# One decoder layer on one core: x handed in by features, without transposes on TensorE

## The chip, the cores and the metric

The kernel runs on one core of a Trainium2 chip. The metric is the device time of one execution in microseconds (us), as the median of several runs. Beside it there is one execution taken by the hardware profiler, with every instruction of every engine: TensorE (PE, with its weight loads as PEld), VectorE (DVE), ScalarE (ACT), GpSimd (POOL) and SyncE (SP). SP, ACT and POOL also issue the transfers between the chip's memory (HBM) and the on-chip memory (SBUF). TensorE writes its products to PSUM.

## What is computed

One layer of a decoder on 512 tokens of width 2048, in float32:

```
h = rmsnorm(x, ln_mix)
proj = h @ w_in                       # 2048 -> 4608: sb_q sb_k sb_v sw_q sw_k sw_v
sb_o = stick_breaking_attention(sb_q, sb_k, sb_v)        # 16 heads, causal
sw_o = sliding_window_sink_attention(sw_q, sw_k, sw_v, sinks, slopes)
x = x + concat(rmsnorm(sb_o, sb_out_norm), rmsnorm(sw_o, swa_out_norm)) @ w_out
gate, up = split(rmsnorm(x, ln_ffn) @ w_gate_up)
x = x + (silu(gate) * up) @ w_down
out = rmsnorm(x, ln_final)
```

with `rmsnorm(x, g) = x * rsqrt(mean(x*x) + 1e-5) * g`. The row factor of the first norm (the rsqrt) is applied late, to the results of the projection; the gain g, one number per feature, is applied early, to x.

## The kernel before

**Products.** Each float32 operand is split into a high part, rounded by a copy on ScalarE, and a low part, the difference, made by VectorE. A product is then three matmuls: high x high, low x high and high x low. For the input the two parts are called hhi and hlo, for the weights whi and wlo.

**x by features.** The first projection contracts over features, so TensorE wants x with features on the 128 partitions: 16 tiles kt of 128 features by 512 tokens. x lies in memory by tokens. `load_x` (line 316) loads it in five chunks of columns (`XC`, line 311; two of 256 columns, three of 512), four transfers each, one for each 128 tokens. `h_make(kt)` (325) lets TensorE transpose four 128 x 128 tiles into one PSUM bank, then `split_scaled` (272) makes hhi (ACT, line 273) and hlo (DVE, line 274) from that bank, multiplied by the gain column `gcol[:, kt]`. `left_sums` (338) forms sums of halves of x that a later product with fewer multiplications needs (the "value pass"): for tiles 0 to 3 and 8 to 11 one sum on POOL from hhi and hlo, and for every tile one or three operations on VectorE that read the PSUM bank; those are put off by one step (`flush`).

**Gains.** `gain_cols` (161) loads the norm weights as rows through ACT's queue, transposes them on TensorE and copies them to `gcol`; once at the start for ln_mix, once later for the other three.

**Sums of squares.** `x_squares(c)` (356) squares a chunk of x, as it was loaded by tokens, on ScalarE with an accumulated sum, after the tiles that need it are transposed.

**Order of the work.** `queue` holds slabs of weights. The first eight (`add_kq`, 560) are the slabs of 256 features by 512 columns of the sliding-window queries; each is 8 groups of three matmuls (lines 569 to 571). `step()` (228) does one group; at the third group of a slab it loads the next two slabs (three buffers "raw") and splits the next (`split`, 205). That runs `prep(s)` first: the h_makes of the tiles in `KTS[s]` (558), so that slab s finds its tiles ready: none for s = 0 (made one by one at the start), then 2, 2, 2, 3, 3 and 2 tiles. whi and wlo have two buffers, so that whi of a slab waits until the slab before last is done. `dma` (99) issues on SP, in program order: x chunk 0, weights 0, x chunk 1, weights 1, chunk 2, and after some steps chunks 3 and 4. Instructions on the engines through `pV`, `pA`, `pG`, `pT` keep program order too and are recorded with line 118.

**At the start** TensorE multiplies a tile of ones with itself (`warm`, 155) until x is there: five before anything else, and eight more between the first transposes.

After the eight slabs comes the value pass, 28 slots of products with the value weights, prepared from line 769 on, and then the attention heads, the output projection and the two large products of the feed-forward part, which take most of the time. Memory of the first phase (`open_phase("p0", 24)`: 24 buffers of 2 KB per partition) is used again by the value pass.

Of the kernel before, what the change touches and what calls it, by code (L numbers as in the profile page):

```python
# [8 lines left out]
F32 = mybir.dt.float32  # L9
# [3 lines left out]
AF = mybir.ActivationFunctionType  # L13
# [3 lines left out]
P = 128  # L17
S = 512
NT = S // P
D = 2048  # L20
# [14 lines left out]


@with_exitstack
def tile_hymba(ctx: ExitStack, tc: tile.TileContext, x, ln_mix, w_in, sb_norm, swa_norm,
               sinks, w_out, ln_ffn, w_gu, w_dn, ln_fin, out):
    nc = tc.nc  # L40
    x2d = x.rearrange("b s d -> (b s) d")
    o2d = out.rearrange("b s d -> (b s) d")
# [2 lines left out]
    const = ctx.enter_context(tc.tile_pool(name="const", bufs=1))  # L45
# [20 lines left out]
    def act8(name, dt=F32R):  # L66
        return act.tile([P, 4, 512], dt, tag="a8", name=name, bufs=8)
# [7 lines left out]
    def pz():  # L75
        return zs[1].tile([P, 512], F32, tag="z", name="z", bufs=4)

    def po():
        return bank("o", 2)

    def four(c):
        return [pz() for _ in range(NT)] if c % 2 == 0 else [pm(), pm(), po(), po()]

    phase = [None, None, 0]

    def open_phase(name, bufs, **kw):
        if phase[0] is not None:
            phase[0].close()
        phase[0] = ExitStack()
        phase[1] = phase[0].enter_context(tc.tile_pool(name=name, bufs=bufs, **kw))  # L90
        phase[2] = bufs
        return phase[1]

    def tmp(dt=F32, name="t"):
        return phase[1].tile([P, 512], dt, tag="t", name=name, bufs=phase[2])

    open_phase("p0", 24)

    def dma(out, in_):
        tc.keep_in_program_order(nc.sync.dma_start(out=out, in_=in_))  # L100

    def f(ap):
        return ap.bitcast(F32)

    mm = nc.tensor.matmul
    V = nc.vector
# [12 lines left out]

    pV, pA, pG, pT = Pinned(V), Pinned(A), Pinned(G), Pinned(nc.tensor)  # L120

    A.preload_act_table_set("natural_log_exp_and_others")

    ident = const.tile([P, P], F32, name="ident")
# [22 lines left out]
                        base=0, channel_multiplier=-1)  # L147
        nc.gpsimd.dma_start(out=sink, in_=sinks[0].partition_broadcast(P))

    gcol = const.tile([P, 48], F32, name="gcol")  # L150


    busy = po()

    def warm(n):
        for _ in range(n):
            pT.matmul(busy[:, 0:P], lhsT=ones, rhs=ones, start=True, stop=True)

    warm(5)

    def gain_cols(rows, c0):
        g = tmp(name="grow")
        n = 0
        for r in rows:
            k = r.shape[0] // P
            nc.scalar.dma_start(out=g[n:n + k, 0:P], in_=r.rearrange("(n p) -> n p", p=P))
            n += k

        def turn():
            pb = pz()  # L170
            nc.tensor.transpose(out=pb[:, 0:n], in_=g[0:n, 0:P], identity=ident[:n, :n])
            V.tensor_copy(out=gcol[:, c0:c0 + n], in_=pb[:, 0:n])
        return turn

    queue = []
    pos = [0, 0]
# [46 lines left out]
    def defer(n, fn):  # L225
        due.append([n, fn])
# [45 lines left out]
    def split_scaled(ps_ap, g_ap, hi, lo):  # L272
        A.activation(out=hi, in_=ps_ap, func=AF.Copy, scale=g_ap)
        V.scalar_tensor_tensor(out=lo, in0=ps_ap, scalar=g_ap, in1=f(hi), op0=ALU.mult, op1=ALU.subtract)
# [32 lines left out]
    h_hi = [None] * KT  # L307
    h_lo = [None] * KT
    h8 = [None, None]
    h8s, vsum, vleft = [], [], {}  # L310
    XC = [(0, 256), (256, 256), (512, 512), (1024, 512), (1536, 512)]
    ss1 = const.tile([P, NT, len(XC)], F32, name="ss1")
    xs = {}
    rs1 = {}

    def load_x(c):
        c0, n = XC[c]
        for t in range(NT):
            xt = tmp(name="xt")[:, 0:n]
            dma(out=xt, in_=x2d[t * P:(t + 1) * P, c0:c0 + n])  # L320
            for k in range(n // P):
                xs[c0 // P + k, t] = xt[:, k * P:(k + 1) * P]
            xs["c", c, t] = xt

    def h_make(kt):
        pb = pz()
        for t in range(NT):
            pT.transpose(out=pb[:, t * P:(t + 1) * P], in_=xs[kt, t], identity=ident)
            warm({(0, 0): 1, (0, 1): 1, (0, 2): 3, (1, 3): 3}.get((kt, t), 0))
        if kt % 4 == 0:  # L330
            h8[0], h8[1] = act8("hhi"), act8("hlo")
        h_hi[kt], h_lo[kt] = h8[0][:, kt % 4, :], h8[1][:, kt % 4, :]
        split_scaled(pb, gcol[:, kt:kt + 1], h_hi[kt], h_lo[kt])
        if kt % 4 == 0:
            h8s.append((h8[0], h8[1]))
        left_sums(kt, pb)

    def left_sums(kt, pb):
        g, j, gc = kt // 8, kt % 4, gcol[:, kt:kt + 1]
        if kt % 8 == 0:  # L340
            vs = [v8.tile([P, 4, 512], F32, tag="v8", name="vs") for _ in range(2)]
            for k, p in enumerate("5736"):
                vleft[g, p] = vs[k // 2][:, :, (k % 2) * 256:(k % 2) * 256 + 256]
        s1, s3, s4, s2 = (vleft[g, p][:, j, :] for p in "5736")
        a, b = pb[:, 0:256], pb[:, 256:512]

        def stt(out, x, y, op):
            pV.scalar_tensor_tensor(out=out, in0=x, scalar=gc, in1=y, op0=ALU.mult, op1=op)

        if kt % 8 < 4:  # L350
            pG.tensor_tensor(out=s1, in0=f(h_hi[kt])[:, 256:512], in1=f(h_lo[kt])[:, 256:512], op=ALU.add)
            vsum.append(lambda: stt(s3, a, s1, ALU.subtract))
        else:
            vsum.append(lambda: (stt(s1, b, s1, ALU.add), stt(s2, b, s3, ALU.subtract), stt(s4, a, s2, ALU.subtract)))

    def x_squares(c):
        for t in range(NT):
            xt = xs["c", c, t]
            pA.activation(out=xt, in_=xt, func=AF.Square, accum_out=ss1[:, t, c:c + 1])

    def rstd1_make():
        sst = sm.tile([P, NT], F32, tag="sst", name="sst")
# [197 lines left out]
    def add_kq():  # L560
        bk = {}

        def one(c, j, s):
            def go(hi, lo):
                k = s * 2 + j
                xh, xl = h_hi[k], h_lo[k]
                wh, wl = hi[:, j, c * P:(c + 1) * P], lo[:, j, c * P:(c + 1) * P]
                o = bk["b"][c]
                mm(o, lhsT=wh, rhs=xh, start=(k == 0), stop=False)
                mm(o, lhsT=wh, rhs=xl, start=False, stop=False)  # L570
                mm(o, lhsT=wl, rhs=xh, start=False, stop=(k == KT - 1))
                if k == KT - 1:
                    if c == 0:
                        kq[0] = const.tile([P, 4, 512], F32, tag="swv", name="kq")
                    if c % 2:
                        A.activation(out=kq[0][:, c, :], in_=o, func=AF.Copy)
                    else:
                        V.tensor_copy(out=kq[0][:, c, :], in_=o)
                return 648.0
            return go  # L580

        def prep(s):
            for kt in KTS[s]:
                h_make(kt)
            defer(1, flush)
            for c in {3: (0, 1), 5: (2,), 6: (3,)}.get(s, ()):
                defer(1, lambda c=c: x_squares(c))

        for s in range(8):
            order = [(c, j) for c in range(4) for j in range(2)] if s == 7 else [(c, j) for j in range(2) for c in range(4)]  # L590
            rows = slice(s * 256, (s + 1) * 256)
            queue.append(dict(srcs=[win[rows, C_SWQ:C_SWQ + 512]], a=2, b=512, big=None,
                              mms=[one(c, j, s) for c, j in order], post=None,
                              pre=(lambda: bk.update(b=four(1))) if s == 0 else None, prep=lambda s=s: prep(s)))
# [72 lines left out]
    def add_swv():  # L667
        def done(t, pb):
            if t == 0:
# [3 lines left out]
        add_tok(lambda s: win[s * 512:(s + 1) * 512, C_SWV:C_SWV + 256], 4, 4, 256, hT,  # L673
                two_m, done, None, True)

    turn1 = gain_cols([ln_mix[0]], 0)
    add_kq()
    load_x(0)
    load(0)
    turn1()  # L680
    load_x(1)
    load(1)
    load_x(2)
    for c in (3, 4):
        while pos[0] < c - 3 or pos[1] < 3:
            step()
        load_x(c)
    turn2 = gain_cols([ln_ffn[0], sb_norm[0], swa_norm[0]], 16)
    defer(8, constants)
    defer(16, turn2)  # L690

    def q_evac(pb, dst):
        V.scalar_tensor_tensor(out=dst, in0=pb, scalar=QSCALE, in1=rs1["b"], op0=ALU.mult, op1=ALU.mult)
# [64 lines left out]
    def drain_to(slab, group):  # L758
        while pos[0] < slab or pos[1] < group:
            step()  # L760
# [6 lines left out]
        vof(n + 2, "to_hp")  # L767

    drain_to(5, 3)
    x_squares(4)  # L770
    open_phase("vp", 1, reuse_waits="tile")
    for n in range(-6, 0):
        if n == -2:
# [1067 lines left out]
    for stage in (0, 1, 2, 4, 3, 5):  # L1841
# [4 lines left out]
    zs[0].close()  # L1846


_INS = ["x", "ln_mix", "w_in", "sb_out_norm", "swa_out_norm", "swa_sinks", "w_out",
        "ln_ffn", "w_gate_up", "w_down", "ln_final"]  # L1850
_OUTS = [((1, 512, 2048), "float32")]


# [19 lines left out]
```

## Time and profile before

| | |
|---|---|
| median of 3 runs | 1988.98 us (1988.75 to 1989.06) |
| the profiled execution | 1988.84 us |
| its span, first to last instruction | 1987.0 us |
| granted TensorE clock, mean | 0.999 of full |
| bytes moved in the span | 252.81 MB |
| the first 58 us: x, eight slabs of query weights | first product at 8.12 us |
| transposes of x on TensorE | 64, from 3.9 to 43.4 us |

A row of a group names the line, the engine, the operation, then the tile it writes, "<-" and those it reads; a number after "x" counts instructions. L118 is the helper that keeps program order, so its rows are told apart by their tiles: `z` is a PSUM bank of the transposes, `xt` a loaded piece of x, `vs` the left sums, `raw` loaded weights, `m` and `o` PSUM banks of products. In the waits, "A <- B: t, n, l" says that A stood idle for t us in n waits, the longest l, until B let it go. An engine with a q is its instruction queue, as SPq for issues of transfers. "Us to landing" counts from the issue of a transfer to its end.

### The profile page before, as it was taken

The numbers are of one execution on the slowest core, as the hardware profiler recorded it, in microseconds if no ns is written. First come the engines' busy times: TensorE is split into PE (matmuls) and PEld (weight loads), VectorE is DVE, ScalarE is ACT, GpSimd is POOL, SyncE is SP. The second block draws the span as 40 slices with busy tenths as digits, with TensorE's granted clock in tenths as the row PEclk, the third lists the DMA queues.
The fourth block names the chain that finished last, engine by engine and source line by source line (L and its number), as shares of the span: only waits on it lengthen the run. The fifth ranks groups of instructions, "written<-read, shape, count | busy, mean of one in ns | idle before, by whom it ended". The sixth has DMA issues, their size and how long they took to land.

```text
span 1987.0 us, 28973 instructions
## 1 busy us (share of the span) xinstructions
PE 1974.1 (99%) x10204; PEld 1687.7 (85%) x10204; DVE 1480.3 (75%) x2053; ACT 1498.5 (75%) x2015; POOL 999.8 (50%) x441
## 2 busy tenths in 40 slices
PE   9999999999999999999999999999999999999998
PEld 8888888898888888888888888888888888888886
DVE  6676888889964787777777777777777867767767
ACT  6775878868753587777777777777777788888887
POOL 2840000000010266657576666657575778878883
PEclk9999999999999999999999999999999999999999
DMA  6415454422342554444545354444534734433523
GB/s 203 148 54 142 97 144 113 121 75 85 96 138 96 172 136 113 127 125 114 137 103 144 101 139 110 129 121 118 135 104 129 279 127 148 149 127 120 177 75 117
DMA packets 290977, 252.81 MB, mean 127 GB/s; under 512 B 12560, under 2 KB 234832, under 8 KB 288400
## 3 DMA queue, kind: packets, MB, share of 16 engines
q1 hardware_dynamic: 289072, 244.11, 42.2%
q0 software_dynamic: 1376, 5.52, 0.9%
q8 instruction: 81, 1.33, 0.3%
q10 hardware_dynamic: 384, 1.34, 0.2%
q14 instruction: 64, 0.52, 0.1%
HBM read 218.40 MB, written 19.92 MB: 120 GB/s over the span
## 4 chain that ended last, share of the span: by engine, by line
PE 97%; ACT 2%; DVE 1%; issue 0%; DVEq 0%; POOL 0%; ACTq 0%; POOLq 0%
PE o L118 36%; PE m L118 30%; PE m L418 3%; PE m L419 3%; PE m L420 3%; PE m L384 2%; PE m L382 2%; PE m L383 2%; PE z L118 1%; PE o L384 1%; PE o L382 1%; PE o L383 1%; PE z L933 1%; PE o L961 1%; PE z L1132 1%; PE z L886 1%
## 5 line engine op out<-in xcount | busy, mean ns | idle before, releaser
L118 DVE TENSOR_TENSOR wlo<-t,hp 128x1024 fp32r<-128x1024 f32 x247 | 301.2, 1219 | 184.6 <-PE o L118 114.2
L118 POOL TENSOR_TENSOR t<-raw,t 128x1024 f32<-128x1024 f32 x111 | 282.2, 2543 | 281.5 <-ACT hp L118 269.6
L118 ACT ACTIVATE whi<-t 128x1024 fp32r<-128x1024 f32 x247 | 262.1, 1061 | 126.4 <-PE o L118 76.4
L118 PE MATMUL o<-hca,whi 128*128 128x512 f32 x880 | 307.5, 391 | 0.0
L118 POOL TENSOR_TENSOR t<-raw,raw 128x1024 f32<-128x1024 f32 x114 | 295.0, 2590 | 21.9 <-issue 11.3
L118 DVE TENSOR_TENSOR wlo<-raw,hp 128x1024 fp32r<-128x1024 f32 x187 | 228.3, 1221 | 93.2 <-issue 52.2
L118 ACT ACTIVATE whi<-raw 128x1024 fp32r<-128x1024 f32 (+1 forms) x189 | 200.0, 1058 | 105.0 <-PE m L118 75.0
L118 ACT ACTIVATE hp<-t 128x1024 fp32r<-128x1024 f32 x247 | 249.2, 1009 | 2.9 <-POOL t L118 2.9
L118 PE MATMUL o<-hca,wlo 128*128 128x256 f32 x880 | 244.0, 280 | 0.0
L118 ACT ACTIVATE hp<-raw 128x1024 fp32r<-128x1024 f32 x191 | 192.9, 1010 | 3.8 <-DVE wlo L118 1.4
L118 PEld LDWEIGHTS o<-hca,whi 128*128 128x128 f32 x880 | 164.2, 187 | 35.8
L118 PE MATMUL m<-hca,whi 128*128 128x512 f32 x528 | 186.3, 392 | 1.1 <-DVE hca L118 1.1
L118 PEld LDWEIGHTS o<-hca,wlo 128*128 128x128 f32 x880 | 165.6, 189 | 0.4
L221 ACT ACTIVATE whi<-raw 128x1024 fp32r<-128x1024 f32 x87 | 91.9, 1057 | 86.1 <-PE o L384 38.6
L222 DVE TENSOR_TENSOR wlo<-raw,whi 128x1024 fp32r<-128x1024 f32 x87 | 109.4, 1258 | 54.7 <-ACT whi L221 52.6
L730 POOL TENSOR_TENSOR sqA<-sqA,oc 128x512 f32<-128x512 f32 x7 | 10.1, 1439 | 273.9 <-ACT oc L729 273.9
L118 PE MATMUL m<-whi,dca 128*128 128x512 f32 x592 | 146.9, 389 | 0.0
L118 PE MATMUL o<-whi,dca 128*128 128x512 f32 x592 | 146.8, 389 | 0.0
L118 PE MATMUL m<-hca,wlo 128*128 128x256 f32 x528 | 146.3, 280 | 0.0
L118 PEld LDWEIGHTS o<-whi,dca 128*128 128x128 f32 x592 | 111.1, 188 | 23.0
L118 PEld LDWEIGHTS m<-whi,dca 128*128 128x128 f32 x592 | 111.0, 188 | 23.1
L118 PE MATMUL m<-hcs,whi 128*128 128x512 f32 x352 | 125.9, 392 | 0.0
(364 smaller groups left out, 5187.5 us busy)
## 6 DMA issues: line engine op xcount, KB each, us to landing
raw<-in_w_gate_up_dram SPq DMA_DIRECT2D x348, 256.0 KB, 5.2
raw<-in_w_down_dram SPq DMA_DIRECT2D x68, 512.0 KB, 5.0
raw<-in_w_in_dram SPq DMA_DIRECT2D x35, 512.0 KB, 4.5
raw<-in_w_in_dram SPq DMA_DIRECT2D x66, 256.0 KB, 3.9
raw<-in_w_out_dram SPq DMA_DIRECT2D x32, 512.0 KB, 3.7
aT<-w SPq DMA_DIRECT2D x44, 256.0 KB, 3.4
xd<-aT SPq DMA_DIRECT2D x10, 1024.0 KB, 6.7
rx<-in_w_down_dram SPq DMA_DIRECT2D x20, 512.0 KB, 5.7
```

Source lines behind the costliest of these rows:

```text
L118: return lambda *a, **k: tc.keep_in_program_order(fn(*a, **k))
L221: A.activation(out=hi, in_=raw, func=AF.Copy)
L222: V.tensor_tensor(out=lo, in0=raw, in1=f(hi), op=ALU.subtract)
L382: mm(o, lhsT=lh[:, sl], rhs=hi[:, j, :], start=first, stop=False, skip_group_check=halves)
L383: mm(o, lhsT=lh[:, sl], rhs=lo[:, j, :], start=False, stop=False, skip_group_check=halves)
L384: mm(o, lhsT=ll[:, sl], rhs=hi[:, j, :], start=False, stop=(k == nslab * a - 1), skip_group_check=halves)
L418: mm(o, lhsT=wh, rhs=xh, start=(k == 0), stop=False)
L419: mm(o, lhsT=wh, rhs=xl, start=False, stop=False)
L420: mm(o, lhsT=wl, rhs=xh, start=False, stop=(k == KT - 1))
L886: mm(out, lhsT=kb, rhs=H.q2[:, c0:S], start=False, stop=True, skip_group_check=True)
L933: mm(zb[:, o:o + r.shape[1]], lhsT=lhsT, rhs=r, start=False, stop=last, skip_group_check=True)
L961: mm(H.ob[:, c0:S], lhsT=vb, rhs=r[:, o:o + S - c0], start=(k == 3 and r is B.h), stop=(k == 0 and r is B.l), skip_group_check=True)
```

## The change

The host hands in two arrays more, which replace the four norm weights: `x_cols`, x transposed (2048 features by 512 tokens), and `gains`, 128 x 48, all four norm weights as columns. x by tokens is still handed in.

- `gcol` is loaded whole by one transfer at the very start, on ACT's queue. `gain_cols`, its two transposes and its copies are gone.
- `load_x` becomes `load_cols(kt, n)`: n tiles of x by features in one transfer on SP's queue (one tile each for 0 and 1, then two at a time), into five buffers.
- `h_make` has no transposes; hhi, hlo and the left sums read the loaded tile in SBUF where they read a PSUM bank.
- `load_rows(t)`: 128 tokens of x, 1 MB, by POOL's queue, four transfers in program order after load_cols(8) to load_cols(14). `x_squares(t)` squares these, in four pieces of 512, put off by one step after the splits of slabs 3 to 6.
- The warming matmuls are ten at the start, and none later.
- Three slabs of weights are loaded ahead of the first step, where it was two, and `constants` is put off from an earlier place.

```
-    open_phase("p0", 24)
+    open_phase("p0", 2)
...
+    gcol = const.tile([P, 48], F32, name="gcol")
+    nc.scalar.dma_start(out=gcol, in_=gains)
     A.preload_act_table_set("natural_log_exp_and_others")
...
-    warm(5)
+    warm(10)
...
+    def load_cols(kt, n):
+        xt = phase[1].tile([P, n, 512], F32, tag="xt", name="xt", bufs=5)
+        dma(out=xt, in_=x_cols[kt * P:(kt + n) * P, :].rearrange("(a p) s -> p a s", p=P))
+        for k in range(n):
+            xs[kt + k] = xt[:, k, :]
+
+    def load_rows(t):
+        xr.append(phase[1].tile([P, D], F32, tag="xr", name="xr", bufs=4))
+        pG.dma_start(out=xr[t], in_=x2d[t * P:(t + 1) * P, :])
 
     def h_make(kt):
-        pb = pz()
-        for t in range(NT):
-            pT.transpose(out=pb[:, t * P:(t + 1) * P], in_=xs[kt, t], identity=ident)
-            warm({(0, 0): 1, (0, 1): 1, (0, 2): 3, (1, 3): 3}.get((kt, t), 0))
+        xt = xs[kt]
...
-        split_scaled(pb, gcol[:, kt:kt + 1], h_hi[kt], h_lo[kt])
+        split_scaled(xt, gcol[:, kt:kt + 1], h_hi[kt], h_lo[kt])
...
-        left_sums(kt, pb)
+        left_sums(kt, xt)
...
-    def x_squares(c):
-        for t in range(NT):
-            xt = xs["c", c, t]
-            pA.activation(out=xt, in_=xt, func=AF.Square, accum_out=ss1[:, t, c:c + 1])
+    def x_squares(t):
+        for k in range(4):
+            xt = xr[t][:, k * 512:(k + 1) * 512]
+            pA.activation(out=xt, in_=xt, func=AF.Square, accum_out=ss1[:, t, k:k + 1])
...
-            for c in {3: (0, 1), 5: (2,), 6: (3,)}.get(s, ()):
-                defer(1, lambda c=c: x_squares(c))
+            if 2 < s < 7:
+                defer(1, lambda: x_squares(s - 3))
...
     add_kq()
-    load_x(0)
+    load_cols(0, 1)
     load(0)
-    turn1()
-    load_x(1)
+    load_cols(1, 1)
+    load_cols(2, 2)
     load(1)
-    load_x(2)
-    for c in (3, 4):
-        while pos[0] < c - 3 or pos[1] < 3:
+    load_cols(4, 2)
+    load(2)
+    load_cols(6, 2)
+    defer(8, constants)
+    for c in range(4, 8):
+        while pos[0] < c - 4 or pos[1] < 3:
             step()
-        load_x(c)
-    turn2 = gain_cols([ln_ffn[0], sb_norm[0], swa_norm[0]], 16)
-    defer(8, constants)
-    defer(16, turn2)
+        load_cols(2 * c, 2)
+        load_rows(c - 4)
...
     drain_to(5, 3)
-    x_squares(4)
```

More of the change, by code (lines that the diff above doesn't have):

```diff
@@ L37, in tile_hymba @@
 @with_exitstack
-def tile_hymba(ctx: ExitStack, tc: tile.TileContext, x, ln_mix, w_in, sb_norm, swa_norm,
-               sinks, w_out, ln_ffn, w_gu, w_dn, ln_fin, out):
+def tile_hymba(ctx: ExitStack, tc: tile.TileContext, x, x_cols, gains, w_in, sinks, w_out, w_gu, w_dn, ln_fin, out):
     nc = tc.nc
@@ L148, in constants @@
         nc.gpsimd.dma_start(out=sink, in_=sinks[0].partition_broadcast(P))
-    gcol = const.tile([P, 48], F32, name="gcol")
     busy = po()
@@ L157, in warm @@
             pT.matmul(busy[:, 0:P], lhsT=ones, rhs=ones, start=True, stop=True)
-    warm(5)
[L161 to L169, printed above, removed]
-            pb = pz()
-            nc.tensor.transpose(out=pb[:, 0:n], in_=g[0:n, 0:P], identity=ident[:n, :n])
-            V.tensor_copy(out=gcol[:, c0:c0 + n], in_=pb[:, 0:n])
-        return turn
+    warm(10)
     queue = []
@@ L310, in tile_hymba @@
     h8s, vsum, vleft = [], [], {}
-    XC = [(0, 256), (256, 256), (512, 512), (1024, 512), (1536, 512)]
-    ss1 = const.tile([P, NT, len(XC)], F32, name="ss1")
-    xs = {}
+    ss1 = const.tile([P, NT, 4], F32, name="ss1")
+    xs, xr = {}, []
     rs1 = {}
-    def load_x(c):
-        c0, n = XC[c]
-        for t in range(NT):
[L319 to L323, printed above, removed]
+    def load_cols(kt, n):
[6 more added lines that the diff above has]
+        pG.dma_start(out=xr[t], in_=x2d[t * P:(t + 1) * P, :])
     def h_make(kt):
-        pb = pz()
-        for t in range(NT):
-            pT.transpose(out=pb[:, t * P:(t + 1) * P], in_=xs[kt, t], identity=ident)
-            warm({(0, 0): 1, (0, 1): 1, (0, 2): 3, (1, 3): 3}.get((kt, t), 0))
+        xt = xs[kt]
         if kt % 4 == 0:
@@ L332, in h_make, with left_sums @@
         h_hi[kt], h_lo[kt] = h8[0][:, kt % 4, :], h8[1][:, kt % 4, :]
-        split_scaled(pb, gcol[:, kt:kt + 1], h_hi[kt], h_lo[kt])
+        split_scaled(xt, gcol[:, kt:kt + 1], h_hi[kt], h_lo[kt])
         if kt % 4 == 0:
             h8s.append((h8[0], h8[1]))
-        left_sums(kt, pb)
-    def left_sums(kt, pb):
+        left_sums(kt, xt)
+    def left_sums(kt, xt):
         g, j, gc = kt // 8, kt % 4, gcol[:, kt:kt + 1]
@@ L344, in left_sums @@
         s1, s3, s4, s2 = (vleft[g, p][:, j, :] for p in "5736")
-        a, b = pb[:, 0:256], pb[:, 256:512]
+        a, b = xt[:, 0:256], xt[:, 256:512]
         def stt(out, x, y, op):
@@ L354, in left_sums @@
             vsum.append(lambda: (stt(s1, b, s1, ALU.add), stt(s2, b, s3, ALU.subtract), stt(s4, a, s2, ALU.subtract)))
-    def x_squares(c):
-        for t in range(NT):
-            xt = xs["c", c, t]
-            pA.activation(out=xt, in_=xt, func=AF.Square, accum_out=ss1[:, t, c:c + 1])
+    def x_squares(t):
+        for k in range(4):
+            xt = xr[t][:, k * 512:(k + 1) * 512]
+            pA.activation(out=xt, in_=xt, func=AF.Square, accum_out=ss1[:, t, k:k + 1])
     def rstd1_make():
@@ L674, in add_swv @@
                 two_m, done, None, True)
-    turn1 = gain_cols([ln_mix[0]], 0)
     add_kq()
-    load_x(0)
+    load_cols(0, 1)
     load(0)
-    turn1()
-    load_x(1)
+    load_cols(1, 1)
+    load_cols(2, 2)
     load(1)
-    load_x(2)
-    for c in (3, 4):
-        while pos[0] < c - 3 or pos[1] < 3:
+    load_cols(4, 2)
[4 more added lines that the diff above has]
+        while pos[0] < c - 4 or pos[1] < 3:
             step()
-        load_x(c)
-    turn2 = gain_cols([ln_ffn[0], sb_norm[0], swa_norm[0]], 16)
-    defer(8, constants)
-    defer(16, turn2)
+        load_cols(2 * c, 2)
+        load_rows(c - 4)
     def q_evac(pb, dst):
@@ L1846, in tile_hymba @@
     zs[0].close()
-_INS = ["x", "ln_mix", "w_in", "sb_out_norm", "swa_out_norm", "swa_sinks", "w_out",
-        "ln_ffn", "w_gate_up", "w_down", "ln_final"]
+_INS = ["x", "x_cols", "gains", "w_in", "swa_sinks", "w_out", "w_gate_up", "w_down", "ln_final"]
 _OUTS = [((1, 512, 2048), "float32")]
@@ L1862 @@
     arrays, args = {}, []
+    inputs["x_cols"] = _np.asarray(inputs["x"])[0].T
+    inputs["gains"] = _np.concatenate([_np.asarray(inputs[n])[0].reshape(-1, P).T for n in
+                                       ("ln_mix", "ln_ffn", "sb_out_norm", "swa_out_norm")], axis=1)
     for name in _INS:
```

## The prediction

> **What bounds the kernel now.** I read the page first, then the waits of TensorE, then the chain of waits over the first 60 us, where everything that the change touches lies.
>
> ```profile
> span 1987.0 us, 28973 instructions
> ...
> PE 1974.1 (99%) x10204; PEld 1687.7 (85%) x10204; DVE 1480.3 (75%) x2053; ACT 1498.5 (75%) x2015; POOL 999.8 (50%) x441
> ...
> PE 97%; ACT 2%; DVE 1%; issue 0%; DVEq 0%; POOL 0%; ACTq 0%; POOLq 0%
> ```
>
> TensorE is busy for 99% of the span and carries 97% of the chain that ended last. The waits of TensorE from 8.2 us to the end are these, the longest first:
>
> ```profile
> PE m L118 <- DVE hca L118: 1.1, 1, 1.1
> PE o L118 <- DVE hct L118: 0.3, 1, 0.3
> PE m L569 <- ACT whi L118: 0.2, 1, 0.2
> ```
>
> No wait after 8.2 us is longer than 1.1 us. So an instruction that leaves TensorE's queue after that shortens the run by its own time, and a new wait of TensorE lengthens it by its own. The chain in order of time (start, length, what) shows which instructions leave:
>
> ```profile
> 1.21 2.50 PE o L118 x10
> ...
> 5.61 1.11 PE o L118 x6
> 6.86 0.69 ACT hhi L273
> 7.55 0.53 ACT whi L118
> 8.12 0.73 PE m L569 x2
> ...
> 9.81 0.88 PE z L118 x8
> 10.68 0.23 PE o L569
> ...
> 16.14 0.87 PE z L118 x8
> ...
> 22.48 0.87 PE z L118 x8
> ...
> 28.81 1.31 PE z L118 x12
> ...
> 35.99 1.31 PE z L118 x12
> ...
> 42.80 0.87 PE z L118 x8
> ```
>
> "PE z L118" are the transposes of x. Until 8.12 us TensorE has no product to do: it transposes the first eight tiles among warming matmuls. From there on the other 56 transposes stand in six blocks between the products, and each block ends where a product begins (9.81 + 0.88 = 10.69, and a product starts at 10.68).
>
> **The change part by part.** Transposes: the six blocks sum to 0.88 + 3 x 0.87 + 2 x 1.31 = 6.11 us, on the path. The turn of the later gains (one small transpose, 0.1 to 0.2 us) goes with them: 0.15. Between the blocks a slab of weights takes 16.14 - 10.68 = 5.46 us for its 24 matmuls; that becomes the period of a slab, where it was 6.3 to 6.8 with a block.
>
> Start: the first product needs one tile of x (now one transfer of 262 KB, first in SP's queue), the gains (ACT's queue), the first half slab of weights, second in SP's queue, and then hhi and whi. Here are the first four issues of SP in the timeline (start, length), and two kinds of transfer with the us from issue to landing:
>
> ```profile
> 0.81 1.81 SPq L100 DMA_DIRECT2D xt<-in_x_dram  x4
> ```
>
> ```profile
> raw<-in_w_in_dram SPq DMA_DIRECT2D x2, 256.0 KB, 4.2
> ...
> grow<-in_ln_mix_dram ACTq DMA_DIRECT2D x1, 8.0 KB, 2.3
> ```
>
> SP issues one transfer per 1.81 / 4 = 0.45 us, so the weights are issued at 1.27, land 4.2 us later at 5.5, and whi (0.53 in the chain) is ready at 6.0. The gains are issued at 0.8 and, at the 2.3 us of the row, come well before; their pieces are of 192 bytes, so I allow them twice that, which is still 5.4 and needs hhi (0.69) behind it: 6.1. The warming matmuls are doubled: ten records took 2.50 us, the next ten at the 1.11 / 6 to 2.50 / 10 of the two rows take 1.9 to 2.5, so they end between 5.6 and 6.2. All three meet near 6.1, and the first product moves from 8.12 to 6.1: 2.0 us gained. Bounds 5.6 and 7.0.
>
> The loads: x now comes twice, by columns through SP (4.19 MB) and by rows through POOL (4.19 MB more), all in the first 35 us. Here are the stretches that matter (length, busy of PE, PEld, DVE, ACT, POOL, clock, DMA share, GB/s):
>
> ```profile
> 2.00:6.00 4.00, 4.00 (x20) 3.74 (x19) 0.17 (x1) 0.09 (x1) 0.91 (x2) 1.00 0.80 205
> 6.00:24.00 18.00, 17.81 (x98) 15.15 (x97) 13.32 (x24) 9.93 (x19) 4.35 (x7) 1.00 1.01 348
> 10.00:48.00 38.00, 38.00 (x196) 31.82 (x195) 30.45 (x56) 24.84 (x59) 8.63 (x11) 1.00 0.59 194
> ```
>
> The transfers are already full from 6 to 24 us (share 1.01, 348 GB/s), but have room over 10 to 48 (share 0.59). So the added rows cost nothing on average, but they can push ahead of weights. Two places are tight.
>
> Slab 1: its weights come behind 2.10 MB in SP's queue, and before they came behind the same 2.10 MB.
>
> ```profile
> 10.77 1.06 ACT L221 ACTIVATE whi<-raw 128x1024 fp32r<-128x1024 f32 x1 [1.60 <-DMA raw<-in_w_in_dram]
> ```
>
> ```profile
> 11.86 1.23 DVE L222 TENSOR_TENSOR wlo<-raw,whi 128x1024 fp32r<-128x1024 f32 x1 [1.67 <-ACT whi L221]
> 13.01 1.40 DVE L274 SCALAR_TENSOR_TENSOR hlo<-z,gcol,hhi 128x512 fp32r<-128x512 f32 x2
> ```
>
> ```profile
> 13.83 1.44 POOL L118 TENSOR_TENSOR vs<-hhi,hlo 128x256 f32<-128x256 f32 x2 [3.05 <-DVE hlo L274]
> ```
>
> whi already waited 1.60 us for them, until 10.77, unseen by TensorE. With issues no longer in the way, 0.82 MB by 6.0 us and the rest at 348 GB/s gives 9.7. From landing to wlo it is 11.86 + 1.23 - 10.77 = 2.3 us, so wlo is ready between 12.0 and 13.1. The third matmul of slab 1 wants it at 6.1 + 5.46 + 0.46 = 12.0. A new stall of 0 to 1.1; I take 0.7, as the row of the same bytes is the nearer.
>
> Slab 4: load_rows(0) stands on POOL behind the left sums of tiles 0 to 3. They ended at 13.83 + 1.44 = 15.27, 7.1 after the first product and with a block between; now that is 6.1 + 7.1 - 0.9 = 12.3. So rows 0 to 2 (3.15 MB) leave together from 12.3 and move, as the first transfers of the run did, some 2 us later, from about 14.5. Behind them on POOL are only the sums of tiles 8 to 11, wanted after 25. On SP 5.77 MB lead up to and include slab 4's weights; 0.82 + 8.5 x 0.348 = 3.78 MB have moved by 14.5, so 1.99 MB must share with the rows. A transfer of 1 MB of x on POOL's queue beside one of weights is in the trace at 487 us (the rate in 40 slices of 487 to 500 us, then the two queues with packets and MB, then the issue):
>
> ```profile
> GB/s 0 0 0 0 0 189 13 25 302 391 429 441 416 416 403 347 391 391 372 277 63 0 0 0 0 0 0 0 0 0 0 0 0 0 0 0 0 0 0 0
> ...
> q0 software_dynamic: 272, 1.05, 26.1%
> q1 hardware_dynamic: 272, 0.52, 11.0%
> ...
> x<-in_x_dram POOLq DMA_DIRECT2D x1, 1024.0 KB, 5.7
> ```
>
> Together the queues lose no rate (391 to 441 GB/s). If they share it evenly, SP has 174 GB/s and the weights land at 14.5 + 1.99 / 0.174 = 25.9. They are wanted 2.3 us ahead of the wlo that slab 4 asks for at 6.1 + 0.7 + 4 x 5.46 + 0.46 = 29.1, so at 26.8: no stall. If POOL's packets (1.05 MB / 272 = 3.9 KB) count as one against SP's (1.9 KB), SP has a third: rows are through at 28.1, the weights at 29.3, a stall of 2.5. I take 0.8, between, nearer to none, since a higher joint rate than 348 is in the row. [...] No run here shows the shares yet.
>
> Waits that are added: load_cols(8) waits for tile 0's part of the left sums on DVE (there are five buffers). It follows hlo of tile 3, which ended at 13.01 + 1.40 = 14.41, 6.3 after the first product, so now near 6.1 + 6.3 - 0.9 + 0.5 = 12.0. Behind it on SP stand all weights from slab 3 on. At that time SP's earlier transfers (3.67 MB) still move until 6 + 2.85 / 0.348 = 14.2, which hides it; without that cover it would cost some 2 us at slab 3. x_squares(t) makes ACT wait for rows t, with the next whi behind it; even sharing brings rows 0 at 20.5. ACT starts slab 3's whi when slab 1 ends, at 6.1 + 0.7 + 2 x 5.46 = 17.7, is free for the squares near 20, and may not start slab 4's whi before slab 2 ends at 23.2. Nothing is lost while ACT has room: it was busy 24.84 us in a stretch that shrinks from 38.0 to 31.9, and its work stays the same. The rest of the program shifts as it is.
>
> The sum against the profiled execution, 1988.84 us (span 1987.0 and 1.84 around it; median of the runs 1988.98): 6.11 + 0.15 + 2.0 - 0.7 - 0.8 = 6.8 gained, **1982.0 us**. All bounds at their good end: 6.1 + 0.2 + 2.5 = 8.8, 1980.0; all at their bad end: 6.1 + 0.1 + 1.1 - 1.1 - 2.5 = 3.7, 1985.1.
>
> **Rivals.** *VectorE becomes the bound.* It works 30.45 of the 38.0 us above and would have 31.9. In the changed kernel its products read x from SBUF and no longer from PSUM. What POOL's sums do beside such work is in the group of the eight and the timeline:
>
> ```profile
> L118 POOL TENSOR_TENSOR vs<-hhi,hlo x8: 737/744/1116, 8.4 to 38.2; 128x256 f32<-128x256 f32 x8
> ```
>
> ```profile
> 8.25 0.68 DVE L118 TENSOR_TENSOR wlo<-raw,whi 128x512 fp32r<-128x512 f32 x1
> ...
> 8.42 2.37 POOL L118 TENSOR_TENSOR vs<-hhi,hlo 128x256 f32<-128x256 f32 x2 [5.50 <-DVE hlo L274]
> ```
>
> The slowest of POOL's eight, 1116 ns against 744, started inside a VectorE subtraction of two SBUF tiles. If the two now shut each other out in all eight cases, and VectorE is the one that waits, it needs 30.45 + 8 x 0.744 = 36.4 us for 31.9: 4.5 us of stall and, without mine, 1988.84 - 8.3 + 4.5 = 1985.0. If POOL waits, nothing changes. [...] Against it: one subtraction a slab, wlo, is of that kind already, and the chain shows no VectorE in this stretch.
>
> *The transfers become the bound, and it is slower.* Before slab 6, ACT must have seen weights 0 to 6 (3.67 MB), columns to tile 13 (3.67) and rows 0 to 2 (3.15), 10.5 MB by 6.1 + 6 x 5.46 - 2.3 = 36.6 us, or 303 GB/s from 2.0. At the two rates of the rows it has 0.82 + 30.6 x 0.348 = 11.5 MB, a margin of 1.0 MB. A gain of 8.3 is eaten up when the 10.5 MB come only at 44.9: the point is a mean of 245 GB/s. At the 205 of the first stretch they would come at 53.2, a stall of 16.6 us and 1997 us; at 220, 13.1 us and **1993.7**. For it: 205 has been measured, over 4 us. Against: 348 and 391 to 441 in the others.
>
> *The blocks were no cost.* If the slabs' period is in truth that of whi, wlo and their buffers (ACT's whi waits for the slab before last to be done), a removed block turns into waiting and only the start is gained: 1988.84 - 2.0 = 1986.8. Against it: whi to wlo take 2.3 us of 5.46.
>
> **How the numbers follow.** About 0.2% (4.0 us) is what a measurement of this kernel can tell from no change, so faster means below 1985.0. The forecast with its bounds has 0.72, VectorE 0.10 (half of it on either side of 1985.0), no cost of the blocks 0.06, slow transfers 0.07, and 0.05 for an order of instructions that comes out otherwise. Faster: 0.72 + 0.05 + 0.03 = 0.80; same 0.13; slower 0.07. The range reaches from 1979.8 to 1985.3: it takes in both ends of the sum and VectorE's case, and leaves out slow transfers and the third rival, 0.13, with what strays.
>
> **What would show each step.** The first product starts near 6.1. No "PE z" of x stands in the chain before 50 us, and a slab takes 5.5 us. Waits of TensorE in slabs 1 and 4 of together some 1.5 us, on whi or wlo behind a transfer of weights. POOL's queue moves 4.2 MB between 14 and 35 us, with the transfers near 100%. The value pass starts near 51 us where it was 58. Wrong it would be if ACT waits for xr for more than 3 us, if VectorE is busy without a gap from 10 to 42 us with TensorE waiting for hlo, or if the slabs stay over 6 us.

## The result and the profile after

| | before | after |
|---|---|---|
| median of 4 runs each, us | 1989.02 (1988.75 to 1989.27) | 2000.07 (1999.10 to 2000.82) |
| the profiled execution, us | 1988.84 | 1999.97 |
| its span, us | 1987.0 | 1998.2 |
| mean granted TensorE clock | 0.999 | 0.995 |

The changed kernel is slower: 1.0055 times the time before, 95% interval 1.0042 to 1.0067, where 0.9965 was forecast. The host makes the two new arrays; the time for that is in none of these numbers. The page after, its span and the chain's shares by engine:

```profile
span 1998.2 us, 28817 instructions
...
PE 94%; DVE 2%; ACT 2%; DMA 1%; issue 1%; SPq 0%; DVEq 0%; ACTq 0%
```

TensorE's share of the chain is down from 97% to 94%. The waits of TensorE from 5 to 70 us (us in all, times, the longest) say for what:

```profile
PE m L550 <- DVE wlo L204: 9.6, 3, 8.3
PE m L548 <- ACT whi L203: 4.6, 1, 4.6
```

Here are TensorE's rows after at the first product, at each of these waits (in brackets the idle time before the row and who ended it), and at the first product of the value pass; then the same first product before:

```profile
5.35 0.48 PE L548 MATMUL m<-hhi,whi 128*128 128x512 f32 x1
...
13.60 0.72 PE L550 MATMUL m<-hhi,wlo 128*128 128x512 f32 x2 [0.77 <-DVE wlo L204]
...
28.46 0.50 PE L548 MATMUL m<-hhi,whi 128*128 128x512 f32 x1 [4.58 <-ACT whi L203]
...
29.72 0.79 PE L550 MATMUL m<-hhi,wlo 128*128 128x512 f32 x1 [0.53 <-DVE wlo L204]
...
62.96 0.79 PE L550 MATMUL m<-hhi,wlo 128*128 128x512 f32 x1 [8.29 <-DVE wlo L204]
...
69.80 1.07 PE L117 MATMUL m<-whi,hhi 128*128 128x512 f32 x4
```

```profile
58.52 1.07 PE L118 MATMUL m<-whi,hhi 128*128 128x512 f32 x4
```

The whole loss is made before the value pass: it starts 69.80 - 58.52 = 11.3 us later, and the span is 11.2 longer. The first product starts 8.12 - 5.35 = 2.8 us earlier and no transpose of x is left, as forecast. But between there and 70 us TensorE stands for 0.77 + 4.58 + 0.53 + 8.29 = 14.2 us, nearly all of it at two places.

**The first stall, slab 3's weights.** SP's, POOL's and ACT's rows after, in three views (start, length, what; for a queue the length reaches from the first of its issues to the end of the last):

```profile
4.81 10.05 SPq L99 DMA_DIRECT2D xt<-in_x_cols_dram  x2
14.96 0.41 SPq L99 DMA_DIRECT2D raw<-in_w_in_dram  x1
```

```profile
14.08 0.55 POOL L117 DMA_DIRECT2D xr<-in_x_dram  x1
...
15.17 1.07 POOL L117 DMA_DIRECT2D xr<-in_x_dram  x2
```

```profile
27.35 1.06 ACT L203 ACTIVATE whi<-raw 128x1024 fp32r<-128x1024 f32 x1 [1.97 <-DMA raw<-in_w_in_dram]
```

SP issues load_cols(6), then stands before load_cols(8) for its buffer and is done with that issue at 14.9. Behind it waits w3, the weights of slab 3, issued at 14.96. By then POOL has begun to issue rows 0 to 2. whi of slab 3 starts only at 27.35, when w3 has come; ScalarE stood idle for it for 1.97 us, and the first of its squares runs behind it, at 28.3. What the transfers did meanwhile (length, busy of PE, PEld, DVE, ACT, POOL, clock, DMA share, GB/s), and the two queues from 16 to 26 us (packets, MB, share of the engines):

```profile
6.00:12.00 6.00, 5.88 (x25) 4.18 (x24) 3.49 (x6) 4.42 (x7) 3.88 (x6) 1.00 1.01 378
12.00:16.00 4.00, 3.23 (x14) 2.35 (x13) 3.82 (x7) 2.97 (x4) 3.96 (x9) 1.00 0.26 57
16.00:30.00 14.00, 8.89 (x38) 6.77 (x37) 7.62 (x14) 3.98 (x8) 0.24 (x1) 0.97 1.01 394
```

```profile
q0 software_dynamic: 402, 2.95, 72.5%
q1 hardware_dynamic: 501, 0.99, 26.0%
```

From 12 to 16 us they had run dry (share 0.26): there was nothing issued to move. From 16 on they are full, but POOL's queue (q0) takes 72.5% and SP's (q1) 26.0%. The packets come out at 402 to 501, nearly one for one, and POOL's are 2.95 MB / 402 = 7.3 KB against 2.0 KB.

**The second stall, the last left sums.** VectorE's last group of left sums with the wlo behind it, POOL's rows beside them, and the group of all left sums on VectorE (ns of the shortest, the median, the longest):

```profile
46.56 13.07 DVE L117 SCALAR_TENSOR_TENSOR vs<-xt,gcol,vs 128x256 f32<-128x256 f32 x6
59.55 3.35 DVE L204 TENSOR_TENSOR wlo<-raw,whi 128x1024 fp32r<-128x1024 f32 x1
```

```profile
46.60 2.69 POOL L117 TENSOR_TENSOR t<-raw,raw 128x1024 f32<-128x1024 f32 x1 [6.88 <-DMA raw<-in_w_in_dram]
49.37 2.48 POOL L117 TENSOR_TENSOR raw<-raw,rx 128x1024 f32<-128x1024 f32 x1
51.79 2.60 POOL L117 TENSOR_TENSOR vf<-vs,vf 128x1024 fp32r<-128x1024 f32 x1
54.35 5.00 POOL L117 TENSOR_TENSOR t<-raw,raw 128x1024 f32<-128x1024 f32 x2
59.42 2.40 POOL L117 TENSOR_TENSOR raw<-raw,rx 128x1024 f32<-128x1024 f32 x1
```

```profile
L117 DVE SCALAR_TENSOR_TENSOR vs<-xt,gcol,vs x32: 471/478/2622, 13.5 to 57.2; 128x256 f32<-128x256 f32 x32
```

The six sums of tiles 14 and 15, 0.48 us each elsewhere, take 13.07 us while POOL prepares the value pass with five sums of 2.4 us and more. VectorE's six start at 46.6, 47.0, 49.6, 52.1, 54.6 and 57.2 us: the first takes 0.48 us, each of the other five 2.44 to 2.62, as long as a whole sum of POOL beside it. The last wlo pays the same (3.35 us, elsewhere 1.2), and TensorE waits 8.29 us for it.

**The clock.** Windows of 2 us after the first stall; the column behind POOL's is the granted clock:

```profile
30.00:32.00 2.00, 2.00 (x5) 1.54 (x6) 2.00 (x5) 2.00 (x7) 0.72 (x1) 0.50 1.06 390
...
36.00:38.00 2.00, 2.00 (x11) 1.62 (x10) 2.00 (x5) 1.61 (x4) 1.23 (x2) 1.00 0.35 54
```

The granted clock falls at 29.1 us, when TensorE has just begun again, and is back at 35.9: for 6.8 us TensorE runs at half its clock (5 matmuls in 2 us, then 11). The prediction had no term for this.

### The profile page after: what moved, and what is told of

It reads as the page before. It is cut to its first block, busy times and chain, and to the rows that moved or that the text cites. A ratio compares the mean times of both kernels' runs of the same rounds, so it can differ in the third digit from the quotient of the medians.

```text
span 1998.2 us, 28817 instructions
## 1 busy us (share of the span) xinstructions
PE 1971.4 (99%) x10132; PEld 1677.1 (84%) x10132; DVE 1496.2 (75%) x2051; ACT 1497.5 (75%) x2007; POOL 1005.0 (50%) x445
## 4 chain that ended last, share of the span: by engine, by line
PE 94%; DVE 2%; ACT 2%; DMA 1%; issue 1%; SPq 0%; DVEq 0%; ACTq 0%
PE o L117 36%; PE m L117 30%; PE m L397 3%; PE m L398 3%; PE m L399 3%; PE m L361 2%; PE m L363 2%; PE m L362 2%; PE o L361 1%; PE o L363 1%; PE o L362 1%; PE z L911 1%; PE z L117 1%; PE o L939 1%; DVE vs L117 1%; DMA raw<-in_w_in_dram 1%
## 5 line engine op out<-in xcount | busy, mean ns | idle before, releaser
L117 DVE TENSOR_TENSOR wlo<-raw,hp 128x1024 fp32r<-128x1024 f32 x187 | 228.3, 1221 | 91.7 <-issue 52.1
L117 PEld LDWEIGHTS o<-whi,dca 128*128 128x128 f32 x592 | 111.1, 188 | 23.1
```

What stands on the lines that cost most here:

```text
L117: return lambda *a, **k: tc.keep_in_program_order(fn(*a, **k))
```

## The experiments

The theory after the result: two causes that do not depend on each other. A, w3 is issued too late and then shares with the rows. B, VectorE's last left sums read two tiles of SBUF, where they read PSUM before, and so stand against POOL's sums of the value pass. A third suspect, C, is the half clock. Rivals to A: ACT, late because of the squares. Rival to B: VectorE simply has too much to do.

**e1_w3_first** (A, half of it): w3 ahead of the load that waits.

```
     load_cols(6, 2)
+    load(3)
```

> One edit to the changed kernel: the weights of slab 3 are issued before columns 8 and 9, whose buffer VectorE frees late. Theory (SP's queue stood behind load_cols(8), ran dry, and slab 3's weights then shared the transfers with three megabytes of rows): the weights land before 16 us, the first long wait of TensorE (4.6 + 0.5 us) goes, and with it the matmuls at half clock behind it (14 x 0.20 = 2.8 us): 8 us less, 1992 us (1990.5 to 1993.5). The second wait, for slab 7's wlo (8.3 us), stays. Rival (the rows alone are too much for the transfers): slab 4 or 5 waits in its place and less than 3 us are won, 1997 or more.

Measured 1996.71 us (1995.65 to 1997.65), ratio to before 1.0038 (1.0024 to 1.0052). TensorE's waits:

```profile
PE m L550 <- DVE wlo L204: 9.8, 3, 8.5
PE m L548 <- ACT whi L203: 1.9, 1, 1.9
```

A miss: 3.4 us won and not 8. Slab 3 no longer waits, but slab 4 does, for w4 and the columns ahead of it, both behind the same rows (the columns come at 28.3, w4 at 29.7), and the half clock follows this shorter stall as well (granted 0.62 from 32 to 36 us). Moving one load moves the stall one slab on and leaves less than half of it.

**e5_thin_rows** (A, the other half): POOL loads 128 columns of the rows and not 2048, and ScalarE squares only these. The kernel leaves out the rest of the sums of squares, so its output is not the layer's.

```
-        pG.dma_start(out=xr[t], in_=x2d[t * P:(t + 1) * P, :])
+        pG.dma_start(out=xr[t], in_=x2d[t * P:(t + 1) * P, 0:P])
```

> The changed kernel with POOL's transfers of x cut to 128 of the 2048 columns and the squares to those columns, so that the sums of squares are incomplete; the order of SP's queue is as it was. It asks which of two causes made slab 3's weights late: that SP stood behind load_cols(8) until 14.9 us, or that the rows then took their share of the transfers (they landed at 27.3). Theory that it takes both: issued at 14.9 as before, the weights land by 21, whi is in time, the first wait (5.1 us) and its half clock (2.8) go, 1992 us (1990.5 to 1993.5), with the wait for slab 7's wlo as it was. Rival that SP's wait alone does it: under 2 us are won, 1998 or more.

Measured 1993.83 us (1993.35 to 1995.33), ratio 1.0027 (1.0016 to 1.0037). ACT's row for whi of slab 3, and TensorE's waits:

```profile
18.58 1.06 ACT L203 ACTIVATE whi<-raw 128x1024 fp32r<-128x1024 f32 x1 [0.16 <-DMA raw<-in_w_in_dram]
```

```profile
PE m L550 <- DVE wlo L204: 10.7, 2, 10.3
```

SP stands as before, but w3 is there at 18.5 and TensorE doesn't wait for it. So the bytes of the rows are what turn SP's standing into a stall; SP's standing alone costs nothing. ACT's squares are made here too, in smaller pieces; that they were not the cause is seen in the kernel after, where the first of them runs behind the late whi. The time is 0.3 us above the range that was expected. One reason is that TensorE, earlier by then, waits 10.3 us at the second place where it waited 8.3: the two losses don't simply add. The other lies far behind both, and is told under e4.

**e2_psum** (B): ScalarE copies tiles 14 and 15 to a PSUM bank, and the left sums read them there.

```
+        if kt > 13:
+            pb = pz()
+            pA.activation(out=pb, in_=xt, func=AF.Copy)
+            xt = pb
         left_sums(kt, xt)
```

> One edit to the changed kernel: for tiles 14 and 15 ScalarE copies x into a PSUM bank (two copies more) and VectorE's left sums read that bank, as in the kernel before. Theory (VectorE with two SBUF inputs and POOL's sums shut each other out, so six left sums of 0.48 us took 13.1 us beside POOL's 2.5 us sums, and slab 7's wlo stood behind them): the six take 2.7 us, the wait of 8.3 us goes, and the half clock behind it (9 x 0.20 = 1.8 us): 10 us less, 1990 us (1988.5 to 1991.5). Rival (VectorE has simply too much to do after the lost time of slab 3): the six still end late, no gain, 1998 or more.

Measured 1989.28 us (1988.46 to 1989.91), ratio 1.0002 (0.9993 to 1.0011). VectorE's row and TensorE's waits:

```profile
47.07 2.69 DVE L117 SCALAR_TENSOR_TENSOR vs<-z,gcol,vs 128x256 f32<-128x256 f32 x6
```

```profile
PE m L552 <- ACT whi L203: 5.9, 1, 5.9
...
PE m L554 <- DVE wlo L204: 0.7, 1, 0.7
```

A hit: the same six sums at the same time, 2.69 us and not 13.07, and the second stall is gone with 10.8 us of the time.

**e4_sbuf_copy** (B against its rival): e1's edit, and the same copy by ScalarE, but into SBUF.

```
-            pb = pz()
+            pb = tmp(name="xc")
```

> The control of the run before: the same two edits, the same copies by ScalarE at the same places, but into SBUF and not into PSUM, so that VectorE's left sums keep two SBUF inputs. Theory (lock by two SBUF inputs): the wait of about 8 us for slab 7's wlo is there as in the run with slab 3's weights first alone: 1992 us (1990 to 1994). Rival (the copy helped by freeing buffers or by delay, not by where VectorE reads): within 1 us of the run with the PSUM bank, 1982.

Measured 1996.63 us (1991.96 to 1998.79), ratio 1.0038 (1.0025 to 1.0051): e1's time. VectorE's row:

```profile
41.78 15.15 DVE L117 SCALAR_TENSOR_TENSOR vs<-xc,gcol,vs 128x256 f32<-128x256 f32 x6
```

The median missed the expectation by 4.6 us because it was reckoned from e1's expected time; against e1's measured one it is 0.1 off. The copy and the number of VectorE's operations are those of e3 below, which takes 12 us less. What decides between the two is the memory that VectorE reads: the six sums take 2.69 us from PSUM in e3 and 15.15 from SBUF in e4.

That 0.1 is in part luck. At the first product of the value pass the profiled execution of e4 (65.10 us) is 1.1 us ahead of e1's (66.22) and 11.8 behind e3's (53.29); from there on, where no edit reaches, it takes some 3 us more than either. Between 800 and 1480 us TensorE gets through fewer matmuls at the same granted clock (length, busy of PE, clock, DMA share, GB/s; e3, then e4):

```profile
800.00:1480.00 680.00, 680.00 (x3917) 1.00 0.46 122
```

```profile
800.00:1480.00 680.00, 680.00 (x3905) 1.00 0.46 122
```

e5 has 3905 too, and loses over 2 us behind the start of the value pass; the eleven other profiled executions have 3916 or 3917. Why is open. So a difference of 2 or 3 us between two runs of this kernel says little until it is known where it arises.

**e3_w3_psum**: e1 and e2 together.

> Both edits: slab 3's weights first, and the left sums of tiles 14 and 15 from PSUM. If the two waits are all that the prediction missed, the gains add: 2000.1 - 8.0 - 10.1 = 1982.0 us (1980.5 to 1983.5), no wait of TensorE over 1 us in the first 70 us, and faster than the kernel before by 7. If something else stands behind the two waits (VectorE as the bound), it shows as waits for wlo or hlo in slabs 4 to 7 and more than 1985.

Measured 1984.30 us (1983.40 to 1987.11), ratio 0.9979 (0.9970 to 0.9989). TensorE's waits:

```profile
PE m L552 <- ACT whi L203: 1.4, 1, 1.4
...
PE m L554 <- DVE wlo L204: 1.0, 2, 0.5
```

Faster than before, but a miss by 2.3 us: w4, with the columns ahead of it, is still late by 1.4 us, and the executions spread over 3.7 us (e4's over 6.8, e9's over 3.8). The granted clock stays at 1.00.

**e7_w3_psum_thin**: e3 with the thin rows.

> The run with both edits (slab 3's weights first, left sums of tiles 14 and 15 from PSUM; 1984.3 us), and POOL's transfers of x cut to 128 columns, so that the sums of squares are incomplete. The waits that were left there stand before slab 4 (1.4 us for whi, 0.5 for wlo). Theory (the rows push slab 4's columns and weights back): they go, and the spread of the runs with them (1983.4 to 1987.1, by the clock after that wait): 1981.5 us (1980.5 to 1982.3). Rival (ACT or VectorE is late by its own work): the waits stay, 1983.5 or more.

Measured 1981.56 us (1980.74 to 1981.96), ratio 0.9962 (0.9947 to 0.9977), a hit. This is the change without its two stalls; the only wait after the first product that the kernel before doesn't have:

```profile
PE m L554 <- DVE wlo L204: 0.6, 1, 0.6
```

**e6_warm** (C): after, with 11 throwaway matmuls of ones ahead of slab 3's first product, to keep TensorE busy.

```
+                if (s, c, j) == (3, 0, 0):
+                    wz = pz()
+                    for _ in range(11):
+                        pT.matmul(wz[:, 0:P], lhsT=ones, rhs=ones, start=True, stop=True)
```

> The changed kernel with eleven matmuls of ones on TensorE ahead of slab 3's first, into a bank that nobody reads: they stand in the first long wait (23.9 to 28.5 us) and would take 11 x 0.43 = 4.7 us of it. Theory (the clock is halved because TensorE stood idle): the granted clock stays 1.0 from 24 to 36 us, the 14 matmuls behind the wait take 0.23 and not 0.43 us each, 2.8 us less, 1997.3 us (1996.5 to 1998.5). Rival (they are slow for another reason, as the transfers are full then): the clock falls to a half as before and the time is 2000 or more.

Measured 1997.81 us (1996.86 to 1999.08), the number expected, but it settles nothing. The row of the throwaway matmuls (two records each):

```profile
22.62 2.62 PE L117 MATMUL z<-ones 128*128 128x128 f32 x22
```

They took 2.62 us, so TensorE still stood for 3.4, and the clock fell to 0.50 within that time. And another thing changed with it: the second wait was 5.1 and not 8.3.

**e9_psum_warm** (C again): e2 with 24 such matmuls.

> As the kernel with the last left sums read from PSUM (1989.28 us), but TensorE makes 24 throwaway matmuls of ones ahead of slab 3's first product, some 0.24 us each, 5.7 us in all, inside the 5.9 us that it waits there for w3. The wait itself stays, since w3 lands as before. If the half clock that follows is the price of standing idle, the granted clock stays at 1.0 from 28 to 36 us, the 14 long matmuls take 0.23 apart and not 0.43, and the time is 1989.3 - 2.8 = 1986.5 us (1985.5 to 1987.5). If the half clock has another cause (the transfers that land then, for one), it stays, and the time is 1989.3 or more.

Measured 1989.98 us (1988.69 to 1992.53), ratio 1.0006 (0.9997 to 1.0016). The throwaway matmuls; two windows; TensorE's waits:

```profile
22.82 5.52 PE L117 MATMUL z<-ones 128*128 128x128 f32 x48
```

```profile
30.00:32.00 2.00, 2.00 (x9) 1.68 (x10) 2.00 (x5) 2.00 (x6) 0.57 (x1) 1.00 1.05 383
...
34.00:36.00 2.00, 1.60 (x8) 0.98 (x6) 2.00 (x3) 2.00 (x7) 1.37 (x2) 1.00 0.03 11
```

```profile
PE m L558 <- DVE wlo L204: 2.1, 3, 0.8
```

Half of each theory holds. The clock stays at 1.00 although the transfers are as full as in e2 (383 GB/s from 30 to 32 us; 384 in e2, where the clock was 0.50), so here the half clock is the price of standing idle. But the 2.8 us are not won: TensorE reaches slab 4 by that much earlier, and waits for wlo once each in slabs 3, 4 and 5 (0.53, 0.75 and 0.83 us). At the first product of the value pass 0.6 us are left (58.99 against 59.59), and in the median nothing. VectorE, which could start wlo of slab 3 only at 28.6, is busy without a gap from 30 to 44 us, as in the two windows, and wlo stands in its queue behind left sums and hlo; ScalarE is as full. So C is hardly a loss of its own at this stall: most of the half clock ran in the shadow of VectorE's backlog, and both are the price of the late w3.

**e8_best**: seven buffers for the columns and three for the rows (the same memory), columns 8 and 9, w3 and columns 10 and 11 issued before the first step, the rows behind the weights on SP's queue, later squares, the constants later and in program order, and e2's copy.

```
     load_cols(6, 2)
+    load_cols(8, 2)
+    load(3)
+    load_cols(10, 2)
+    defer(16, constants)
...
-        pG.dma_start(out=xr[t], in_=x2d[t * P:(t + 1) * P, :])
+        dma(out=xr[t], in_=x2d[t * P:(t + 1) * P, :])
```

> A version meant to keep the gain: the rows go through SP's queue behind the weights of the slab that is wanted first, columns 8 to 11 and slab 3's weights are issued ahead, columns have seven buffers and rows three, the squares come one slab later, the left sums of tiles 14 and 15 read a PSUM bank, and the constants keep their place behind the first left sums. If the waits of TensorE found so far are all, the sum of the prediction without its two stalls holds: 2.8 for the start (first product at 5.4), 6.1 for the blocks, 0.15 for the turn: 1988.9 - 9.0 = 1979.9 us (1979 to 1981.5), with no wait of TensorE over 0.5 us in the first 60 us. If the squares, now later, block ACT, whi of slab 6 or 7 is late and it is 1982 or more.

Measured 1982.86 us (1982.74 to 1983.38), ratio 0.9970 (0.9958 to 0.9981): a miss by 3 us, and not because of the squares. One wait was left, for wlo, 1.6 us of the 3, and POOL's row shows why:

```profile
23.92 6.07 POOL L117 TENSOR_TENSOR vs<-hhi,hlo 128x256 f32<-128x256 f32 x3 [9.19 <-DVE hlo L256]
```

Three of POOL's short left sums of tiles 8 to 11 (0.74 us each in the kernel before, by the median) take 6.07 us, the longest 4.5, beside a VectorE without a gap from 21.1 to 27.8 us; a left sum of VectorE then waits for the result. Here it is POOL that is held up.

**e10_best2**: all eight of POOL's left sums on ScalarE.

```
-            pG.tensor_tensor(out=s1, in0=f(h_hi[kt])[:, 256:512], in1=f(h_lo[kt])[:, 256:512], op=ALU.add)
+            pA.activation(out=s1, in_=b, func=AF.Copy, scale=gc)
```

> As the best version so far (1982.86 us; weights of slab 3 ahead, rows behind the weights on SP's queue, last left sums from PSUM), but the left sums of tiles 0 to 3 and 8 to 11 of the first pass are scaled by ScalarE and no longer by POOL, which in the version before took up to 4.5 us for one of them beside VectorE. If POOL and VectorE shut each other out there, the last wait of 1.6 us goes: 1982.9 - 1.6 = 1981.3 us (1980 to 1982.5). If ScalarE, which gets eight more operations of some half a microsecond, becomes late with the weights' high halves, it is 1982.9 or more.

Measured 1984.29 us (1982.18 to 1984.97), ratio 0.9975 (0.9965 to 0.9985): no gain. The wait for wlo is gone, but an equal one stands at 10.4 us (the profile is of the fastest of the eight executions, 1982.18 us; what the others lost beyond it isn't seen):

```profile
PE m L552 <- ACT whi L117: 1.6, 1, 1.6
```

ACT's row ahead of that whi, POOL's issue of a small table, and the transfers beside it:

```profile
8.70 0.72 ACT L255 ACTIVATE hhi<-xt,gcol 128x512 fp32r<-128x512 f32 x1 [3.24 <-DMA xt<-in_x_cols_dram]
```

```profile
1.94 0.72 POOL L149 DMA_DIRECT2D sink<-in_swa_sinks_dram  x1
```

```profile
5.00:6.00 1.00, 1.00 (x5) 1.00 (x5) 0.84 (x2) 0.45 (x1) 0.00 (x0) 1.00 0.77 50
```

Only a little of this is ScalarE's doing (a left sum of 0.49 us ahead of whi). POOL, with nothing to wait for, issued the 8 KB load of the constants at 1.9 us and not behind its first left sums at 9.3. Between 5 and 6 us the transfers then moved 50 GB/s, where e8 has 363, and x's second tile came at 8.7. That the small load caused the drop is argued from the order, not shown by a run that moves it alone. In e11 below, where it is issued at 9.5 us again, the transfers move 332 GB/s from 5 to 6 us.

**e11_best3**: e8 with only tiles 8 to 11 on ScalarE, so that POOL keeps its first sums ahead of that load.

> As the best version (1982.86 us), with only the left sums of tiles 8 to 11 moved from POOL to ScalarE, not those of tiles 0 to 3. In the version with all eight moved, TensorE's wait of 1.6 us behind VectorE was gone, but one of 1.6 us stood at 10.4 us instead, where ScalarE had a left sum of tiles 0 to 3 ahead of a high half of weights. If the two waits are that cheaply told apart, both go: 1982.9 - 1.6 = 1981.3 us (1980 to 1982.3). If the spread of the executions (1982.2 to 1985.0 in that version) has a cause outside of these waits, the median stays at 1982.9 or above although the profile shows no wait.

Measured 1980.61 us (1979.86 to 1983.04), ratio 0.9962 (0.9948 to 0.9976): the expected number, though the expectation put the wait at 10.4 us down to ScalarE's order, where the trace puts most of it down to the late tile. Neither wait is left. Of the versions that compute the whole layer it is the fastest, 0.4% under the kernel before and 1.0% under the change as it was made.

## Why the prediction was wrong

The spans of four profiled executions take the result apart: before 1987.0, e7 1979.8, e2 1988.2, after 1998.2.

- **The change without its stalls, 1987.0 - 1979.8 = 7.2 us gained.** The prediction's gains, 6.11 + 0.15 + 2.0 = 8.3, were of the right kind. The gain columns (`gcol`) landed 3.1 us after their issue, where the prediction allowed twice 2.3; the doubling was a margin of the author's that no run shows. The first product came at 5.35, even earlier than 6.1, and at 5.50 in e7. There the value pass starts at 51.02, as predicted ("near 51 us"), but that is partly luck: the 51 held two stalls of together 1.5 us and the later start. What is missing of the gains is the 0.6 that e7 still waits and a rest that was not pursued. e7 leaves out most of the squares; that this is not where the gain comes from is seen in e11, which makes all of them and has a span of 1978.3.
- **The step that failed first: "which hides it".** The prediction saw that load_cols(8) would wait and that all weights from slab 3 on stand behind it, and let transfers that "still move until 14.2" hide the wait. They were all but through at 12: they ran at 378 GB/s where 348 was taken, and from 2 to 6 us at over 300 where the sum had 205. The buffer came free near 14.4 and not 12.0, since the first left sum on VectorE started only at 13.46 and took 0.96 beside a sum of POOL. So the queue ran dry for 4 us. The price quoted for that case, "some 2 us at slab 3", left out that w3 would then be issued beside the rows. With the half clock behind it, this stall costs 8.4 us (e2 to e7, which has both w3 ahead and the rows out of the way).
- **The share of the two queues was mis-sized.** The prediction took it from a place where POOL's packets were 3.9 KB, which gave SP a third at worst, and went on "nearer to none". The rows' packets were 7.3 KB and SP got 26%: of the two queues 402 and 501 packets moved from 16 to 26 us. So the end of the range that counted packet against packet was the one to take here, with the packet size of this very transfer.
- **The step that failed second: "The rest of the program shifts as it is".** It does not. The left sums had read PSUM, and their last six stand beside the first sums of the value pass on POOL. Rival one had the mechanism and found the slow sum in the trace, but priced eight POOL sums of 0.744 us. The prediction looked for POOL's work only where the change touched POOL. The sums that counted were 2.4 us long, and VectorE waited one out for nearly each of its six: 10.0 us (e2 to after) for 0.48 us operations. Against the rival it was said that wlo is of that kind already; wlo is one operation a slab, and the last left sums are six in a row.
- **VectorE and POOL.** e2 against after, and e3 against e4, show the delay: the same sums from PSUM take 2.69 us and from SBUF 13.07 and 15.15. Three sums on POOL that take 6.07 us in e8 are the other side of it. What in the chip makes the two wait for each other, no run here shows.
- **Slab 1 had the stall that was priced at 0.7, and it was 0.77, but not for the weights.** VectorE had waited for one of POOL's constants ahead of wlo. A right number with a wrong reason.
- **The rivals.** Transfers had no lack of rate (394 GB/s from 16 to 30 us): rival two's place was right and its mechanism wrong, as the rate was there but went to the rows. Blocks that cost nothing: excluded by e7. ACT did not wait for rows at all.

Taken together: 1987.0 - 7.2 + 8.4 + 10.0 = 1998.2. These are differences along one order of edits; e5 shows that in another order the parts have other sizes. By the medians of the same four they are 7.5, 7.7 and 10.8 us, since e2's profiled execution is 0.6 above its median.

What stays open: why the executions of e3, e4 and e9 spread over 3.7 us and more (in e3 not by the mean granted clock: 1986.39 us has 0.999, 1983.50 has 0.998; whether it is the slower stretch that e4 and e5 show can't be seen, as only one execution of each has a profile), what the half clock after the second stall costs by itself, and whether the drop in e10 is the small load's.

## What to carry to other kernels

When an operand moves from PSUM to SBUF, list every operation of VectorE that now has two inputs in SBUF, and look at what POOL does beside each of them, in the next stage too; price each at one whole operation of POOL (here 0.48 us became 2.44 to 2.62). When a wait is added ahead of a load, ask what will be issued on other queues by the time it ends, and take the share by the packet sizes of those very transfers (here 7.3 KB against 2.0 KB, and 72.5% against 26.0%). A wait "hidden" by two microseconds of transfers is hidden only if the rate is no better than you took it for (here 378 GB/s, where 348 was taken).

## What the runs showed of the hardware

- VectorE and POOL held each other up: six sums of 0.48 us took 13.07 (after) and 15.15 us (e4) beside POOL when they read x in SBUF, and 2.69 us from PSUM (e2, e3); a sum on POOL of 0.74 us (its median before) took up to 4.5 us beside a VectorE without gaps (e8).
- Two full queues moved 402 and 501 packets in 10 us (after, 16 to 26 us): packets of 7.3 KB got 72.5%, those of 2.0 KB 26.0%.
- After 4.6 us of idle TensorE ran at half its clock for 6.8 us (after); kept busy with throwaway matmuls in e9 it kept its clock (1.00 from 22 to 44 us). The fall has no fixed distance from the last matmul: 5.2 us in the kernel after (23.9 to 29.1), 2.2 us in e2 (23.1 to 25.3). The stretches at half clock in this part of the kernel are 3.4 us (e1, e4), 6.8 (after and e6, twice each) or 10.2 long (e1, e2, e4, e5), in these runs whole multiples of 3.4. In e1 the clock fell after 1.95 + 0.53 us of idle with two matmuls between, and in e3 it did not after 1.44 + 0.53. How long an idle time it takes, these runs do not show.
